# Gate and up products of a SwiGLU layer as Strassen block products, with the activations split later

## The chip, the cores and the metric

The kernel runs on one core of one Trainium2 chip. The metric is the time of one execution on the device, in microseconds (us). TensorE (PE in the rows) multiplies; VectorE (DVE), ScalarE (ACT) and GpSimd (POOL) work element by element; SyncE (SP) issues the loads of the weights.

## The reference, cut to what matters

One encoder layer over 512 tokens, model width 1024, inner width 2816, all in float32:

```python
h = h + 0.5 * swiglu(rms_norm(h, ffn1_norm), ffn1_w_gate, ffn1_w_up, ffn1_w_down)
u = rms_norm(h, mix_norm) @ w_in                  # 1024 -> 1280
...                                               # window attention and pooling on u
h = h + concat([a, p]) @ w_out
h = h + 0.5 * swiglu(rms_norm(h, ffn2_norm), ffn2_w_gate, ffn2_w_up, ffn2_w_down)
out = rms_norm(h, final_norm)

def swiglu(x, w_gate, w_up, w_down):
    return (silu(x @ w_gate) * (x @ w_up)) @ w_down
```

The change touches the two products `x @ w_gate` and `x @ w_up` of both FFNs, and how their result is handed to `w_down`.

## The kernel before

Every product is made from three matmuls in a 32-bit format of TensorE's that keeps fewer bits than float32 (fp32r in the rows). Each operand is split into a high part (a cast to that format, on ScalarE) and a low part (the rest, a subtraction on VectorE), and `mm3` (line 113) adds high times high, high times low and low times high into the same PSUM bank. Activations lie transposed, features on the 128 partitions and the 512 tokens along the free axis, so one matmul is 128x128 weights against 128x512 activations.

The weights come as a stream of *units* of 1 MB (a list `units`, line 56). `load` brings a unit into one of two `raw` buffers; `split_next` makes of each half of it, a *piece* of 1024 columns, the pair `wh`, `wl` (lines 97 and 98), in four buffers each; `weights()` hands out the next piece and keeps two more asked for. The code is run once to write the program down; each engine then takes its instructions strictly in its own order and waits by semaphores, and that order comes from the order of the code and a scheduler that may move an instruction ahead.

An FFN has two stages. In `gate_up` (line 202) the first three of the 22 column tiles (`F0 = 3`, each 128 inner columns of gate and of up) are done side by side over the eight blocks of the input as these become ready; this is the *head*, eight steps of 18 matmuls. At its end `norm_sums` (line 183) and `norm_spread` (line 197) make `rstd`, the factor of the RMS norm per token. Then follow 19 tiles of 2 x 8 x 3 = 48 matmuls each. The norm's factor is put in after the product: `glu` (line 203) multiplies the gate's bank by `rstd` on VectorE (line 206), takes the sigmoid on ScalarE (207), multiplies on GpSimd (208), multiplies the up bank in on VectorE (209) and `rstd` on GpSimd (210); then it splits the activation into high (ScalarE, 212) and low (GpSimd, 213), and both parts of all 22 tiles are kept. In `down` (line 250) each of the 22 blocks of `w_down` meets the kept parts in eight banks, 24 matmuls per block.

Between the two FFNs lies the mixing stage (projections, attention, pooling), which the change does not touch. Attention's scores are the only matmuls before that are 256 columns wide (lines 518 and 519).

Of the kernel before, what the change touches and what calls it, by code (L numbers as in the profile page):

```python
# [8 lines left out]
F32 = mybir.dt.float32  # L9
# [27 lines left out]
def encoder_layer(ctx: ExitStack, tc: tile.TileContext, xT, w1h, w1gu, w1d, win, wout, w2h, w2gu, w2d,  # L37
# [20 lines left out]
    units += [(w2gu, i) for i in range(NF - F0)] + [(w2d, i) for i in range(NF // 2)]  # L58
    stream = {"asked": 0, "raw": None, "ready": []}

    early = {}

    def load(i, between=None):
        src, j = units[i]
        n = src.shape[-1] // 2
        if i in early:
            return early.pop(i)
        raw = wts.tile([P, 2048], F32, name="raw", tag="raw", bufs=2)
        if i == 0:
# [6 lines left out]
        return raw, n  # L76

    def split_next():

        i, half = stream["asked"] // 2, stream["asked"] % 2  # L80
        if i == len(units):
            return
        if half == 0 and i:
            stream["raw"] = load(i)
        raw, n = stream["raw"]
        src = raw[:, half * n:(half + 1) * n]
        spare = stream.get("spare")
        if spare:
            wh, wl = spare.pop(0)
# [3 lines left out]
        m = n // 2 if stream["asked"] == 0 else n  # L93
        on_pool = WIN_POOL if units[i][0] is win else WOUT_POOL if units[i][0] is wout else ()
        sub = nc.gpsimd if 2 * units[i][1] + half in on_pool else nc.vector
        for c in range(0, n, m):
            nc.scalar.copy(wh[:, c:c + m], src[:, c:c + m])  # L97
            sub.tensor_tensor(wl[:, c:c + m], src[:, c:c + m], wh[:, c:c + m].bitcast(F32),  # L98
                              op=ALU.subtract)
        stream["asked"] += 1  # L100
        stream["ready"].append((wh, wl))

    def weights(ahead=2):
        while len(stream["ready"]) <= ahead and stream["asked"] < 2 * len(units):
            split_next()
        return stream["ready"].pop(0)
# [24 lines left out]

    stream["raw"] = load(0, start)
    nc.vector.memset(ones, 1.0)
# [3 lines left out]
    keep_awake(ps, WARM)  # L137
    early[1] = load(1)
    xload(4, 5, 6, 7)
# [60 lines left out]


    def gate_up(xh, xl, act, tmp, after_first, before=None, each=None):
        def glu(f, pg, pu):
            t1 = tmp.tile([P, S], F32, name="t1", tag="t1", bufs=2)
            t2 = tmp.tile([P, S], F32, name="t2", tag="t2", bufs=2)
            nc.vector.tensor_tensor(t1, pg, rstd, op=ALU.mult)  # L206
            nc.scalar.activation(t2, t1, AF.Sigmoid)  # L207
            nc.gpsimd.tensor_tensor(t2, t2, t1, op=ALU.mult)  # L208
            nc.vector.tensor_tensor(t1, pu, t2, op=ALU.mult)  # L209
            nc.gpsimd.tensor_tensor(t1, t1, rstd, op=ALU.mult)  # L210
            ah, al = act(f)
# [20 lines left out]
        after = after_first()  # L232
        for f in range(F0, NF):
            pb = []
            for u in range(2):
                wh, wl = weights()
                ps = bank()
                for k in range(KD):
                    c = slice(k * P, (k + 1) * P)
                    mm3(ps, wh[:, c], wl[:, c], xh[:, k, :], xl[:, k, :], k == 0, k == KD - 1)  # L240
                    if f == F0 and u == 0 and k == 4:
                        norm_spread(after)
                        for j in range(F0):
                            glu(j, banks[j], banks[F0 + j])
                pb.append(ps)
            glu(f, pb[0], pb[1])
            if each is not None:
                each(f)

    def down(act, tokens_first, finish):  # L250

        banks = [bank() for _ in range(8)]

        def one(i, k, wh, wl, last):
            ah, al = act(k)
            if tokens_first:
# [5 lines left out]

        kept, hold = [], 4 if tokens_first else 2
        for k in range(NF):
            if tokens_first and stream["asked"] == 2 * len(units) - 2:
                w2 = base.tile([P, 4, 1024], F32R, name="w2", tag="xl")
                stream["spare"] = [(w2[:, 0, :], w2[:, 1, :]), (w2[:, 2, :], w2[:, 3, :])]
            wh, wl = weights()
            if k < NF - hold:
                for i in range(8):  # L270
                    one(i, k, wh, wl, False)
            else:
                kept.append((k, wh, wl))
        for i in range(8):
            for k, wh, wl in kept:
                one(i, k, wh, wl, k == NF - 1)
            finish(i, banks[i])


    with tc.tile_pool(name="ffn1", bufs=1) as fp:  # L280
        a1h = fp.tile([P, NF, S], F32R, name="a1h")
        a1l = fp.tile([P, NF, S], F32R, name="a1l")

        def first_norm(k):

            norm_in(0, k, xh, xl)
            if k >= LAG:
                squares(k - LAG)

        def first_sums():  # L290
            for k in range(KD - LAG, KD):
                squares(k)
            return norm_sums()

        gate_up(xh, xl, lambda f: (a1h[:, f, :], a1l[:, f, :]), fp, first_sums,
                before=first_norm)
        yh = base.tile([P, KD, S], F32R, name="yh", tag="xh")
        yl = base.tile([P, KD, S], F32R, name="yl", tag="xl")

        def finish1(i, ps):  # L300
            nc.vector.scalar_tensor_tensor(h[:, i, :], ps, 0.5, h[:, i, :], op0=ALU.mult, op1=ALU.add)
            norm_in(1, i, yh, yl)

        down(lambda f: (a1h[:, f, :], a1l[:, f, :]), False, finish1)

# [330 lines left out]

    with tc.tile_pool(name="ffn2", bufs=1) as fp:
        FB = NF - 4
        a2h = fp.tile([P, FB, S], F32R, name="a2h")
        a2l = fp.tile([P, FB, S], F32R, name="a2l")  # L640
        hT = fp.tile([P, NT, D], F32, name="hT")
        late = []

        def after_first():
            spread = norm_sums()
            return spread

        def turn_h(f):
            if f <= F0:
                return  # L650
            if f - F0 - 1 < 2 * NT:
# [141 lines left out]
```

## Time and profile before

| | |
|---|---|
| time, median of 3 runs (lowest to highest) | 891.41 us (889.97 to 891.98) |
| the profiled execution's own time | 891.37 us |
| its span in the trace | 889.6 us |
| TensorE busy | 98% of the span, 3918 matmuls |
| VectorE, ScalarE, GpSimd busy | 46%, 35%, 35% |
| weights read | 82 MB, 95 GB/s over the span |

The span runs from the first to the last instruction that the profiler saw; the time of the execution is 1.8 us longer. "Busy" for TensorE counts matmuls in flight, which overlap. In the rows an instruction stands as start, duration, engine, line, operation and tiles (output <- inputs), and in brackets the idle time ahead of it and what ended that.

### The profile page before, as it was taken

How to read it: one execution, taken by the hardware profiler on the slowest of the kernel's cores; microseconds unless marked ns; L12 is line 12 of the kernel's file. 1: busy time of each engine (PE TensorE's matmuls, PEld its weight loads, DVE VectorE, ACT ScalarE, POOL GpSimd, SP SyncE). 2: the span in 40 equal slices, each digit the busy share in tenths (PEclk: the TensorE clock that was granted, in tenths of full speed). 3: DMA queues.
4: the chain of work that ended last, by engine and by line, in shares of the span. 5: the costliest groups of instructions: out<-in, count | busy, mean ns of one | idle time of the engine just before them, and what ended most of it. 6: DMA issues, size and time to landing. Idle time of an engine off the chain costs nothing.

```text
span 889.6 us, 9675 instructions
## 1 busy us (share of the span) xinstructions
PE 872.2 (98%) x3918; PEld 719.3 (81%) x3918; DVE 408.4 (46%) x516; ACT 309.9 (35%) x454; POOL 311.8 (35%) x255
## 2 busy tenths in 40 slices
PE   8999999999999999999789999999999999999996
PEld 7888888888888888887668888888888888888885
DVE  6444444444432221669887643444444444322225
ACT  7353222333321111543666532533323322211223
POOL 5186444444420001855542220763444444200004
PEclk9999999999999999999999999999999999999998
DMA  6422222222222222221211123122222222332202
GB/s 237 156 81 95 95 97 98 102 106 101 104 102 95 95 95 95 84 95 50 97 44 36 61 93 125 66 95 95 94 95 95 95 94 95 127 104 104 105 11 94
DMA packets 14683, 84.79 MB, mean 95 GB/s; under 512 B 1824, under 2 KB 2352, under 8 KB 5808
## 3 DMA queue, kind: packets, MB, share of 16 engines
q1 hardware_dynamic: 13104, 81.60, 25.8%
q10 hardware_dynamic: 1440, 2.57, 0.9%
q8 instruction: 30, 0.49, 0.2%
q14 instruction: 13, 0.11, 0.0%
q0 software_dynamic: 96, 0.02, 0.0%
HBM read 82.08 MB, written 2.10 MB: 95 GB/s over the span
## 4 chain that ended last, share of the span: by engine, by line
PE 92%; DVE 4%; ACT 1%; POOL 1%; issue 1%; DMA 0%; DVEq 0%; POOLq 0%; ACTq 0%
PE ps L114 29%; PE ps L115 29%; PE ps L116 29%; DVE qq L391 1%; PE ps L547 1%; DVE wl L98 1%; PE ps L563 1%; PE ps L562 1%; DVE rtmp L359 1%; DMA small<-in_gains 0%; PE ps L655 0%; DVE u L360 0%; PE ps L226 0%; PE ps L228 0%; PE ps L198 0%
## 5 line engine op out<-in xcount | busy, mean ns | idle before, releaser
L98 DVE TENSOR_TENSOR wl<-raw,wh 128x1024 fp32r<-128x1024 f32 (+2 forms) x146 | 215.6, 1478 | 206.2 <-ACT wh L97 197.7
L97 ACT CAST wh<-raw 128x1024 fp32r<-128x1024 f32 (+2 forms) x153 | 156.3, 1024 | 415.1 <-PE ps L115 339.3
L114 PE MATMUL ps<-zh,wh 128*128 128x512 f32 x346 | 135.5, 392 | 0.0
L115 PE MATMUL ps<-zl,wh 128*128 128x512 f32 x346 | 135.1, 390 | 0.0
L116 PE MATMUL ps<-xh,wl 128*128 128x512 f32 x346 | 135.0, 391 | 0.0
L114 PE MATMUL ps<-xh,wh 128*128 128x512 f32 x346 | 134.8, 390 | 0.0
L116 PE MATMUL ps<-zh,wl 128*128 128x512 f32 x346 | 134.8, 390 | 0.0
L115 PE MATMUL ps<-xl,wh 128*128 128x512 f32 x346 | 134.6, 389 | 0.0
L208 POOL TENSOR_TENSOR t<-t,t 128x512 f32<-128x512 f32 x44 | 77.7, 1769 | 146.0 <-ACT t L207 146.0
L210 POOL TENSOR_TENSOR t<-t,rstd 128x512 f32<-128x512 f32 x44 | 61.2, 1394 | 99.3 <-DVE t L209 99.3
L209 DVE TENSOR_TENSOR t<-ps,t 128x512 f32<-128x512 f32 x44 | 30.4, 691 | 120.2 <-PE ps L116 108.2
L114 PEld LDWEIGHTS ps<-xh,wh 128*128 128x128 f32 x346 | 64.9, 188 | 13.9 <-ACT wh L97 0.2
L116 PEld LDWEIGHTS ps<-zh,wl 128*128 128x128 f32 x346 | 64.9, 188 | 13.9 <-issue 0.2
L116 PEld LDWEIGHTS ps<-xh,wl 128*128 128x128 f32 x346 | 64.9, 188 | 14.0 <-issue 0.2
L115 PEld LDWEIGHTS ps<-zl,wh 128*128 128x128 f32 x346 | 65.0, 188 | 13.4 <-issue 0.2
L115 PEld LDWEIGHTS ps<-xl,wh 128*128 128x128 f32 x346 | 65.0, 188 | 13.4
L114 PEld LDWEIGHTS ps<-zh,wh 128*128 128x128 f32 x346 | 65.0, 188 | 13.2
L206 DVE TENSOR_TENSOR t<-ps,rstd 128x512 f32<-128x512 f32 x44 | 30.2, 691 | 92.3 <-PE ps L116 75.9
L114 PE MATMUL ps<-a1h,wh 128*128 128x512 f32 x176 | 68.5, 389 | 0.0
L115 PE MATMUL ps<-a1l,wh 128*128 128x512 f32 x176 | 68.5, 389 | 0.0
L116 PE MATMUL ps<-a1h,wl 128*128 128x512 f32 x176 | 68.5, 389 | 0.0
L98 POOL TENSOR_TENSOR wl<-raw,wh 128x1024 fp32r<-128x1024 f32 x7 | 16.8, 2396 | 117.3 <-ACT wh L97 114.3
(189 smaller groups left out, 1270.2 us busy)
## 6 DMA issues: line engine op xcount, KB each, us to landing
raw<-in_w1gu SPq DMA_DIRECT2D x19, 1024.0 KB, 4.7
raw<-in_w2gu SPq DMA_DIRECT2D x19, 1024.0 KB, 4.7
raw<-in_w1d SPq DMA_DIRECT2D x11, 1024.0 KB, 4.7
raw<-in_w2d SPq DMA_DIRECT2D x11, 1024.0 KB, 4.8
raw<-in_win SPq DMA_DIRECT2D x5, 1024.0 KB, 4.7
raw<-in_wout SPq DMA_DIRECT2D x4, 1024.0 KB, 4.8
raw<-in_w2h SPq DMA_DIRECT2D x4, 768.0 KB, 4.2
raw<-in_w1h SPq DMA_DIRECT2D x3, 768.0 KB, 4.3
```

The source lines that it names most:

```text
L97: nc.scalar.copy(wh[:, c:c + m], src[:, c:c + m])
L98: sub.tensor_tensor(wl[:, c:c + m], src[:, c:c + m], wh[:, c:c + m].bitcast(F32), op=ALU.subtract)
L114: nc.tensor.matmul(ps, lhsT=ah, rhs=bh, start=start, stop=False)
L115: nc.tensor.matmul(ps, lhsT=ah, rhs=bl, start=False, stop=False)
L116: nc.tensor.matmul(ps, lhsT=al, rhs=bh, start=False, stop=stop)
L206: nc.vector.tensor_tensor(t1, pg, rstd, op=ALU.mult)
L208: nc.gpsimd.tensor_tensor(t2, t2, t1, op=ALU.mult)
L209: nc.vector.tensor_tensor(t1, pu, t2, op=ALU.mult)
L210: nc.gpsimd.tensor_tensor(t1, t1, rstd, op=ALU.mult)
L359: nc.vector.tensor_tensor(rot, rot, sr, op=ALU.mult)
L391: nc.vector.scalar_tensor_tensor(t[o, :], u[r, :], -HD ** -0.5, t[r, :].bitcast(F32), op0=ALU.mult, op1=ALU.subtract)
L547: nc.tensor.transpose(ps[:, i * P:(i + 1) * P], sc[g][0][:, i, (b - lo) * P:(b - lo + 1) * P], ident)
```

## The change

For 37 of the 38 later tiles (18 in FFN1, where one tile stays as it was, and 19 in FFN2; the constant `PLAIN`) the gate and up columns of one tile are taken as a 2x2 block product: the weights in four blocks of 512 rows by 128 columns (a11 and a12 are gate's two halves of the input rows, a21 and a22 up's), the activations in four blocks of 512 rows by 256 tokens. Strassen's scheme in Winograd's form needs seven block products where the plain way needs eight. A block product is 4 x 3 matmuls of 128x128 weights against 128x256 activations, so a tile has 84 matmuls of 256 columns in place of 48 of 512.

- The four sums of the weights are made per tile in a buffer `sums`, of which there is one: three on GpSimd (lines 106, 107 and 111), one on VectorE (114). A unit now gives four pieces (three of 1024 columns, one of 512) to cast and subtract.
- The four sums of the input are made once per FFN, in `combine`, four rounds of two products with gain and `rstd` on VectorE (line 248), four subtractions on GpSimd (251), one cast of 1792 columns on ScalarE (252) and one subtraction of the same width on VectorE (253). Its buffer has the tag of `sums`. So that `rstd` is there in time, `norm_sums` and `norm_spread` move into the head (`norm_steps`).
- The seven products are added up by four instructions on VectorE that read PSUM (lines 320, 323, 326 and 330) and a copy on ScalarE (316). The activation is one SiLU on ScalarE and one product on GpSimd (333).
- The activations are kept whole, and `down` splits each block two ahead of its use, on ScalarE and VectorE (lines 391 and 392).

```diff
+            a11, a12, a21, a22 = (raw[:, c * 512:(c + 1) * 512] for c in range(4))
+            if part == 0:
+                stream["sums"] = stream["pool"].tile([P, 2048], F32, name="sums", tag="sums")
+            s2, s1, s3, s4 = (stream["sums"][:, c * 512:(c + 1) * 512] for c in range(4))
+            n = 512 if part == 3 else 1024
+            if part == 0:
+                nc.gpsimd.tensor_tensor(s1, a21, a22, op=ALU.add)
+                nc.gpsimd.tensor_tensor(s3, a11, a21, op=ALU.subtract)
+                src = raw[:, 0:1024]
+            elif part == 1:
+                load(i + 1)
+                nc.gpsimd.tensor_tensor(s2, s1, a11, op=ALU.subtract)
+                src = stream["sums"][:, 0:1024]
+            elif part == 2:
+                nc.vector.tensor_tensor(s4, a12, s2, op=ALU.subtract)
+                src = stream["sums"][:, 1024:2048]
+            else:
+                src = a22
...
+        def combine(j):
+
+            b = gp.tile([P, 2048], F32, name="tt", tag="sums").rearrange("p (b c) -> p b c", b=8)
+            for k, o in ((j, b[:, 0:8:7, :]), (j + KD // 2, b[:, 1:3, :])):
+                nc.vector.scalar_tensor_tensor(o, halves(h[:, k, :]), gain[:, n, k:k + 1], halves(rstd),
+                                               op0=ALU.mult, op1=ALU.mult)
+            for o, x, y in ((3, 7, 0), (5, 2, 7), (4, 2, 3), (6, 1, 4)):
+                nc.gpsimd.tensor_tensor(b[:, o, :], b[:, x, :], b[:, y, :], op=ALU.subtract)
+            nc.scalar.copy(th[:, j, :, :], b[:, 0:7, :])
+            nc.vector.tensor_tensor(tl[:, j, :, :], b[:, 0:7, :], th[:, j, :, :].bitcast(F32),
+                                    op=ALU.subtract)
...
+        def product(w, side, t, ps):
+            for j in range(KD // 2):
+                c = slice(side * 512 + j * P, side * 512 + (j + 1) * P)
+                mm3(ps, w[0][:, c], w[1][:, c], th[:, j, t, :], tl[:, j, t, :], j == 0, j == KD // 2 - 1)
+
+        for f in range(F0 + PLAIN[0 if n == 0 else 1], NF):
+
+            c = parts()
+            b0, b1 = halves(bank()), halves(bank())
+            w = weights()
+            product(w, 0, 0, b0[:, 0, :])
+            p1 = gp.tile([P, 1, HF], F32, name="p1", tag="p1")
+            nc.scalar.copy(p1[:, 0, :], b0[:, 0, :])
+            product(w, 1, 1, b1[:, 0, :])
+            w = weights()
+            product(w, 0, 4, b1[:, 1, :])
+            nc.vector.tensor_tensor(c[:, 0:6:5, :], b1, p1.to_broadcast([P, 2, HF]), op=ALU.add)
+            v = weights()
+            product(v, 0, 5, b0[:, 1, :])
+            nc.vector.tensor_tensor(c[:, 4, :], b0[:, 1, :], c[:, 5, :], op=ALU.add)
+            b2, b3 = halves(bank()), halves(bank())
+            product(w, 1, 3, b2[:, 0:1, :])
+            nc.vector.tensor_tensor(c[:, 3:7:3, :], c[:, 4:6, :], b2[:, 0:1, :].to_broadcast([P, 2, HF]),
+                                    op=ALU.add)
+            product(v, 1, 2, b3[:, 1, :])
+            product(weights(), 0, 6, b3[:, 0, :])
+            nc.vector.tensor_tensor(c[:, 1:3, :], b3, c[:, 4:7:2, :], op=ALU.add)
+            t2 = pair("t2")
+            nc.scalar.activation(halves(t2), c[:, 0:4:2, :], AF.Silu)
+            nc.gpsimd.tensor_tensor(halves(act(f)), c[:, 1:4:2, :], halves(t2), op=ALU.mult)
+            each(f)
...
+        ab[0], ab[1] = split(0), split(1)
         for k in range(NF):
             wh, wl = weights()
+            if 0 < k < NF - 1:
+                ab[k + 1] = split(k + 1)
...
+            nc.scalar.copy(ah, act(k))
+            nc.vector.tensor_tensor(al, act(k), ah.bitcast(F32), op=ALU.subtract)
```

Below, the four pieces of a tile are called 0 to 3 in the order of the code, the sums s1 to s4 as in the code, the VectorE instructions that add up the products c1 to c4 in the order of the code (lines 320, 323, 326, 330). The products run in the order t = 0, 1, 4, 5, 3, 2, 6; piece 0 serves the first two, piece 1 the third and fifth, piece 2 the fourth and sixth, piece 3 the last.

VectorE's order, before, over two tiles in the middle of FFN1 (names with a number are `glu`'s buffers):

```order
L206 TENSOR_TENSOR t_1076<-ps,rstd 128x512
L98 TENSOR_TENSOR wl<-raw,wh 128x1024
L209 TENSOR_TENSOR t_1076<-ps,t_1077 128x512
L98 TENSOR_TENSOR wl<-raw,wh 128x1024
L206 TENSOR_TENSOR t_1145<-ps,rstd 128x512
L98 TENSOR_TENSOR wl<-raw,wh 128x1024
L209 TENSOR_TENSOR t_1145<-ps,t_1146 128x512
L98 TENSOR_TENSOR wl<-raw,wh 128x1024
```

The same engine now, from one tile's c1 to the next one's (`parts` holds the tile's partial sums, `p` with a number is the copy p1):

```order
L320 TENSOR_TENSOR parts<-ps,p_1245 128x2x256
L323 TENSOR_TENSOR parts<-ps,parts 128x256
L326 TENSOR_TENSOR parts<-parts,ps 128x2x256
L126 TENSOR_TENSOR wl<-sums,wh 128x1024 x2
L330 TENSOR_TENSOR parts<-ps,parts 128x512
L126 TENSOR_TENSOR wl<-raw,wh 128x512
L114 TENSOR_TENSOR sums<-raw,sums 128x512
L126 TENSOR_TENSOR wl<-raw,wh 128x1024
L320 TENSOR_TENSOR parts<-ps,p_1366 128x2x256
```

Four instructions per tile became nine: c1 to c3 of a tile, then pieces 1 and 2 of the next tile, c4, piece 3 of the next tile, then s4 and piece 0 of the tile after that.

GpSimd's order, before, over two tiles of FFN1:

```order
L208 TENSOR_TENSOR t_870<-t_870,t_869 128x512
L210 TENSOR_TENSOR t_869<-t_869,rstd 128x512
L213 TENSOR_TENSOR a1l<-t_869,a1h 128x512
L208 TENSOR_TENSOR t_939<-t_939,t_938 128x512
L210 TENSOR_TENSOR t_938<-t_938,rstd 128x512
L213 TENSOR_TENSOR a1l<-t_938,a1h 128x512
```

And now (`late_xh` holds the kept activations):

```order
L106 TENSOR_TENSOR sums<-raw 128x512
L107 TENSOR_TENSOR sums<-raw 128x512
L111 TENSOR_TENSOR sums<-sums,raw 128x512
L333 TENSOR_TENSOR late_xh<-parts,t_1343 128x512
L106 TENSOR_TENSOR sums<-raw 128x512
L107 TENSOR_TENSOR sums<-raw 128x512
L111 TENSOR_TENSOR sums<-sums,raw 128x512
```

Three instructions per tile became four, and the product of the activation stands behind the three sums of a later tile.

VectorE's order now where FFN1's input is summed, after the head (L248 and L253 are `combine`; L258, L263 and L392 belong to the head's activations):

```order
L248 SCALAR_TENSOR_TENSOR tt<-h,small,rstd 128x2x256
L248 SCALAR_TENSOR_TENSOR tt<-h,small,rstd 128x512
L263 TENSOR_TENSOR parts<-ps,t_399 128x512
L258 TENSOR_TENSOR parts<-ps,rstd 128x512
L392 TENSOR_TENSOR as_2557<-some,as_2557 128x512 x2
L253 TENSOR_TENSOR tl<-tt,th 128x1792
L263 TENSOR_TENSOR parts<-ps,t_493 128x512
L114 TENSOR_TENSOR sums<-raw,sums 128x512
L126 TENSOR_TENSOR wl<-sums,wh 128x1024 x2
L126 TENSOR_TENSOR wl<-raw,wh 128x512
L248 SCALAR_TENSOR_TENSOR tt<-h,small,rstd 128x2x256
L248 SCALAR_TENSOR_TENSOR tt<-h,small,rstd 128x512
```

These are the second round and the start of the third; the first block tile's weight sums, which use the same buffer, stand between them.

## Rows read from the trace of the kernel before

**Rows 1.** The page's first part: busy time, share of span, instructions.
```profile
PE 872.2 (98%) x3918; PEld 719.3 (81%) x3918; DVE 408.4 (46%) x516; ACT 309.9 (35%) x454; POOL 311.8 (35%) x255
```

**Rows 2.** Timeline, one tile of FFN1: VectorE, then GpSimd (start us, duration us).
```profile
101.67 0.69 DVE L206 TENSOR_TENSOR t<-ps,rstd 128x512 f32<-128x512 f32 x1 [2.23 <-PE ps L116]
102.57 1.23 DVE L98 TENSOR_TENSOR wl<-raw,wh 128x1024 fp32r<-128x1024 f32 x1 [0.21 <-ACT wh L97]
107.18 0.69 DVE L209 TENSOR_TENSOR t<-ps,t 128x512 f32<-128x512 f32 x1 [3.38 <-PE ps L116]
108.02 2.30 DVE L98 TENSOR_TENSOR wl<-raw,wh 128x1024 fp32r<-128x1024 f32 x1
112.55 0.69 DVE L206 TENSOR_TENSOR t<-ps,rstd 128x512 f32<-128x512 f32 x1 [2.23 <-PE ps L116]
...
107.95 1.29 POOL L210 TENSOR_TENSOR t<-t,rstd 128x512 f32<-128x512 f32 x1 [3.00 <-DVE t L209]
109.97 1.49 POOL L213 TENSOR_TENSOR a1l<-t,a1h 128x512 fp32r<-128x512 f32 x1 [0.73 <-ACT a1h L212]
```

**Rows 3.** Timeline of TensorE in the mixing stage: matmuls of 256 columns.
```profile
467.95 0.28 PE L518 MATMUL ps<-kk,qq 128*128 128x256 f32 x1
...
468.43 0.39 PE L114 MATMUL ps<-pdh,wh 128*128 128x512 f32 x1
```

**Rows 4.** Timeline of FFN1's head: VectorE, then GpSimd.
```profile
19.30 1.09 DVE L98 TENSOR_TENSOR wl<-raw,wh 128x768 fp32r<-128x768 f32 x1 [0.87 <-ACT wh L97]
20.32 2.04 DVE L98 TENSOR_TENSOR wl<-raw,wh 128x768 fp32r<-128x768 f32 x1
...
19.66 1.88 POOL L171 TENSOR_TENSOR acc<-acc,sq 128x512 f32<-128x512 f32 x1
```

**Rows 5.** Timeline after FFN1's head: VectorE with a PSUM operand, then GpSimd.
```profile
59.30 0.68 DVE L209 TENSOR_TENSOR t<-ps,t 128x512 f32<-128x512 f32 x1
...
56.99 3.53 POOL L208 TENSOR_TENSOR t<-t,t 128x512 f32<-128x512 f32 x2 [0.20 <-ACT t L207]
```

**Rows 6.** Groups by line and shape: count, busy us, mean ns, idle before.
```profile
L98 POOL TENSOR_TENSOR wl<-raw,wh 128x1024 fp32r<-128x1024 f32 x7 | 16.8, 2396 | 117.3 <-ACT wh L97 114.3 <-PE ps L114 3.0
L403 DVE TENSOR_TENSOR vv<-ps,vv 128x256 fp32r<-128x256 f32 x2 | 0.8, 410 | 0.0
L97 ACT CAST wh<-raw 128x1024 fp32r<-128x1024 f32 x136 | 143.0, 1052 | 398.3 <-PE ps L115 325.9 <-PE ps L116 65.8 <-POOL acc L171 3.5
L97 ACT CAST wh<-raw 128x768 fp32r<-128x768 f32 x15 | 12.3, 835 | 14.7 <-PE ps L115 13.4 <-PE ps L226 0.7 <-DMA raw<-in_w1h 0.5
```

**Rows 7.** Timeline of VectorE: 512 columns, both operands in SBUF.
```profile
419.32 0.68 DVE L359 TENSOR_TENSOR rtmp<-rtmp,sr 128x512 f32<-128x512 f32 x1
```

**Rows 8.** Timeline, marks of both FFNs: two head steps (VectorE), then TensorE.
```profile
28.58 1.23 DVE L98 TENSOR_TENSOR wl<-raw,wh 128x1024 fp32r<-128x1024 f32 x1 [2.29 <-ACT wh L97]
32.66 1.23 DVE L98 TENSOR_TENSOR wl<-raw,wh 128x1024 fp32r<-128x1024 f32 x1 [2.85 <-ACT wh L97]
...
39.77 0.95 PE L187 MATMUL ps<-ones,acc 128*128 128x1 f32 x8
248.35 0.39 PE L114 MATMUL ps<-a1h,wh 128*128 128x512 f32 x1
517.82 0.39 PE L224 MATMUL ps<-zh,wh 128*128 128x512 f32 x1
551.27 0.49 PE L114 MATMUL ps<-zh,wh 128*128 128x512 f32 x1
762.91 0.39 PE L114 MATMUL ps<-wh,a2h 128*128 128x512 f32 x1
```

**Rows 9.** Timeline of TensorE at the start of attention's scores, after a wait.
```profile
430.32 0.39 PE L518 MATMUL ps<-kk,qq 128*128 128x256 f32 x1 [2.49 <-DVE qq L391]
...
431.31 0.63 PE L115 MATMUL ps<-yl,wh 128*128 128x512 f32 x1
431.74 0.63 PE L116 MATMUL ps<-yh,wl 128*128 128x512 f32 x1
```

More of the change, by code (lines that the diff above doesn't have):

```diff
@@ L58, in encoder_layer @@
     units += [(w2gu, i) for i in range(NF - F0)] + [(w2d, i) for i in range(NF // 2)]
-    stream = {"asked": 0, "raw": None, "ready": []}
-    early = {}
+    pieces = []
+    for i, (src, j) in enumerate(units):
+        if (src is w1gu and j >= PLAIN[0]) or (src is w2gu and j >= PLAIN[1]):
+            pieces += [("block", i, part) for part in range(4)]
+        else:
+            pieces += [("half", i, 0), ("half", i, 1)]
+    stream = {"asked": 0, "ready": []}
+    raws = {}
     def load(i, between=None):
+        if i in raws or i == len(units):
+            return
         src, j = units[i]
         n = src.shape[-1] // 2
-        if i in early:
-            return early.pop(i)
         raw = wts.tile([P, 2048], F32, name="raw", tag="raw", bufs=2)
-        if i == 0:
+        raws[i] = raw
+        if between is not None:
             for q in range(4):
@@ L103, in weights @@
     def weights(ahead=2):
-        while len(stream["ready"]) <= ahead and stream["asked"] < 2 * len(units):
+        while len(stream["ready"]) <= ahead and stream["asked"] < len(pieces):
             split_next()
@@ L130, in start @@
         xload(*((0,), (1,), (2,), (3,))[q])
-    stream["raw"] = load(0, start)
+    load(0, start)
     nc.vector.memset(ones, 1.0)
@@ L240, in gate_up, with down @@
                     mm3(ps, wh[:, c], wl[:, c], xh[:, k, :], xl[:, k, :], k == 0, k == KD - 1)
[L241 to L244, printed above, removed]
                 pb.append(ps)
[L246 to L250, printed above, removed]
+                after(KD + u, combine)
+            glu_up(f, pb[1], *glu_gate(pb[0]))
+        def product(w, side, t, ps):
[27 more added lines that the diff above has]
+            each(f)
+    def down(split, tokens_first, finish, ready=None):
         banks = [bank() for _ in range(8)]
+        ab = {}
         def one(i, k, wh, wl, last):
-            ah, al = act(k)
+            ah, al = ab[k]
             if tokens_first:
@@ L273, in down @@
                 kept.append((k, wh, wl))
+        if ready is not None:
+            ready()
         for i in range(8):
@@ L277, in down, with inner, act, split @@
             finish(i, banks[i])
+    def inner(first, pool, place):
+        some = pool.tile([P, 6, S], F32, name="some")
+        late, done = {}, {}
+        def act(f):
+            if f < 6:
+                return some[:, f, :]
+            t = ("xh", "xl")[(f - 6) // 8]
+            if t not in late:
+                late[t] = base.tile([P, 8, S], F32, name="late_" + t, tag=t)
+            return late[t][:, (f - 6) % 8, :]
+        def split(k, where=None):
+            if k in done:
+                return done[k]
+            if k < 2:
+                if "place" not in done:
+                    done["place"] = place()
+                ah, al = (done["place"][:, 2 * k + c, :] for c in range(2))
+            else:
+                t = where.tile([P, 2, S], F32R, name="as", tag="as", bufs=6)
+                ah, al = t[:, 0, :], t[:, 1, :]
+            nc.scalar.copy(ah, act(k))
+            nc.vector.tensor_tensor(al, act(k), ah.bitcast(F32), op=ALU.subtract)
+            done[k] = ah, al
+            return done[k]
+        return act, split
@@ L280, in encoder_layer @@
     with tc.tile_pool(name="ffn1", bufs=1) as fp:
-        a1h = fp.tile([P, NF, S], F32R, name="a1h")
-        a1l = fp.tile([P, NF, S], F32R, name="a1l")
+        act1, split1 = inner(True, fp, lambda: fp.tile([P, 4, S], F32R, name="as0"))
         def first_norm(k):
[L286 to L296, printed above, removed]
@@ L634, in encoder_layer @@
             weave(project_out(d, ath, atl, finish_attn), [])
[L637 to L640, printed above, removed]
+    with ExitStack() as two:
+        fp = two.enter_context(tc.tile_pool(name="ffn2", bufs=1))
         hT = fp.tile([P, NT, D], F32, name="hT")
[L642 to L646, printed above, removed]
+        act2, split2 = inner(False, fp, lambda: base.tile([P, 4, S], F32R, name="as0", tag="h"))
         def turn_h(f):
```

139 lines of the change are left out of this document (87 added, 52 removed).

## The prediction

> **What bounds the kernel now.** I read the busy shares first: TensorE 98%, the three element-wise engines 35 to 46% [rows 1]. Then one tile: the same VectorE line comes at 101.67 and 112.55 [rows 2], so a tile takes 10.88 us, and 48 matmuls in 10.88 us are 0.227 us each. TensorE sets the pace, and the others wait for it (the brackets name PE). Then I read how VectorE and GpSimd stand to each other, since the change puts its additions there. At 108.02 a 1024-column subtraction with both operands in SBUF takes 2.30 us in place of the 1.23 us of 102.57: GpSimd had begun 0.07 us before it and held until 109.24, and 1.08 us later VectorE was done. The other way round, GpSimd's line 213 begins at 109.97 and ends at 111.46, 1.14 us after VectorE's end at 110.32, where line 210 alone takes 1.29 [rows 2]. So two such instructions do not overlap at all; one waits until the other has ended. Back to back they take turns: VectorE's two of 19.30 and 20.32 let GpSimd's in between, which ends 21.54 (1.15 after 20.39), and the second ends 0.82 after that [rows 4]. An instruction of VectorE with a PSUM operand is free of this: 0.68 us at 59.30 inside a pair of GpSimd's [rows 5].
>
> **TensorE's part.** Per block tile 48 matmuls of 512 go and 84 of 256 come. Four of 256 columns, each with its own weights, start within 467.95 to 468.43 [rows 3], 0.120 each; half of 0.227 would be 0.113. I take 0.118, so 84 x 0.118 = 9.9 us (bounds 9.5 and 10.1): 1.0 us less per tile, 37 us over 37 tiles, if nothing else sets the pace. The Trainium skill (TensorE: Matmul & The Clock Gate, Back-to-back issue gap) gives 262 cycles at full clock for 256 columns, 0.109 us, which would make the tile 9.2 us; its 518 cycles for 512 are 0.216, where this trace has 0.227, so the rows are taken; by the page's figure rival (a) below would be 25 us shorter and the forecast the same.
>
> **The tile on VectorE and GpSimd.** There is one buffer `sums`. s1 of the next tile but one can start only when the subtraction of piece 2 has read it, and VectorE's order ties the rest: s4 needs s2, piece 0 stands behind s4, c1 to c3 behind piece 0, pieces 1 and 2 behind c3. That is a ring, and it turns once per tile. Its prices: GpSimd, 512 columns, 1.29, or 1.14 after a wait for VectorE [rows 2]; VectorE, 1024 columns, 1.23 with a pitch of 1.14 (estimate: 0.08 of the next overlaps, as 20.32 begins 0.07 before 20.39 [rows 4]), 512 columns in SBUF 0.68 [rows 7], 0.54 after a wait (half of 1.08), c1 and c3 like the 0.69 of line 209 [rows 2], c2 the 0.41 of 256 columns [rows 6]. From the end of piece 2:
> s1 0.08 + 1.29; piece 3, which waited for s1, 0.54; s3, which waited for piece 3, 1.14; s2 1.29; then the product of the activation, next on GpSimd and long ready, 1.29; s4, which waited for that, 0.54; piece 0 1.14; c1, c2, c3 0.69 + 0.41 + 0.69; pieces 1 and 2 1.14 + 1.23. Sum **11.47**; some steps overlap by hundredths and I take **11.4 us** per tile. c4 runs beside s1 and costs nothing. TensorE's products for c1 to c3 are long done by then: the third begins when piece 1 is ready, a whole turn ahead. So the ring is 1.5 us longer than TensorE's 9.9, and longer than the old 10.88. Lower bound 10.9, with every GpSimd step at 1.14; upper 11.7, with 0.08 more at each handoff.
>
> **The start of each FFN.** A round of `combine`: two products with two SBUF operands, 2 x 0.68; four GpSimd subtractions of 256 columns, not in the trace: from 1.29 at 512 and 2.40 at 1024 [rows 2, 6] the line gives 0.74, half of 1.29 gives 0.65, I take 0.74 and 2.96; a cast of 1792, by the line through 0.84 and 1.05 at 768 and 1024 [rows 6], 1.70; a subtraction of 1792, by the line through 0.68 and 1.23 [rows 2, 7], 2.05. With handoffs 8.2 us, and since the rounds share the one buffer they follow each other: 33 us (bounds 28 and 38).
> FFN1: a head step is 4.08 us [rows 8], two before the head's end at 39.77 are left after the sums, so the spread is done at 37.4 and `rstd` at 38.4. Rounds from 39, 33 us, and between the second and third the first block tile's sums and pieces (3 x 1.29, 0.68, 2.3 and a cast ahead, 8 us), and 1 us of the head's own work: the last round ends at 81. By the order 44 of the tile's 84 matmuls need it: 5.2 us, the first block tile ends at **86**. Before, 17 tiles of 10.88 end at 248.35 [rows 8], so that one ended at 63.4: 23 us lost. Tile two's sums begin at 81 (same buffer); its piece 2 is ready 10.3 us later (3 x 1.29, s4, three pieces, c1 to c4), four products follow, 5.7 us: **97**. Sixteen more tiles: 97 + 16 x 11.4 = 279.4 against 248.35, **+31**.
> FFN2: there is no plain tile as cover. Sums after two head steps, spread after three, `rstd` at 517.82 + 14.8 = 532.6. Rounds to 567; s1, s3, a product of the head's, s2, s4, piece 1: 574; five products, 7.1: the first block tile ends at **581** where the old one ended about 562.5 (551.27 [rows 8] + 10.88 and 0.4 of the norm's spread). The second, whose sums follow at once, at 588; 17 more: 588 + 17 x 11.4 = 781.8 against 762.91 [rows 8], **+19**.
>
> **What hides.** The split in `down`: 0.62 (the casts' line at 512) and 0.68 per block beside 5.44 us of TensorE, with 1.05 and 1.23 there already; GpSimd is idle there, so nothing is waited for. If that cover went it would be 44 x 0.7 us = 31 us. Loads: a raw buffer is free one turn ahead of its need. c4, SiLU, the copy p1: beside the ring. The moved sums of the norm: the same matmuls, elsewhere. I take 0 for these, with -2 to +4.
>
> **Sum.** 889.6 + 31 + 19 = 939.6 us of span, 941.4 with the 1.8 us around it; the profiled execution (891.37) is the median's (891.41) within 0.1 us. Forecast **941**, its own range 920 (ring 10.9, 33 turns, -16; starts -5) to 957 (ring 11.7, +10; starts +6).
>
> **Rivals.** (a) *The ring does not bind.* If VectorE and GpSimd overlap here as they do with PSUM [rows 5], the ring loses piece 3's 0.54 and the product's 1.29, comes to 9.8, and TensorE's 9.9 sets the tile; the starts stay. FFN1 86 + 17 x 9.9 = 254.3 (+6); FFN2 581 + 18 x 9.9 + 4 for the transposes of h that stand between the tiles (762.91 - 551.27 is 4.9 more than 19 x 10.88) = 763 (0): **897**. For it: only pairs of VectorE and GpSimd were seen, not the new shapes. Against: no two-SBUF pair in the rows overlaps.
> (b) *Faster.* The rounds hide too, because the first tile's products start on the rounds that are done. Then 37 x 1.0 us come off: **857**. It decides from the point at which the last round ends before TensorE has run out of plain work (52 us in FFN1, 552 in FFN2); by the sum it ends at 81 and 567, so both rounds' prices would have to halve.
> (c) *Slower still, by the clock.* After a wait of 2.49 us TensorE's matmuls of 512 stand 0.43 apart, which is 1.2 GHz, where they stood 0.23 apart before [rows 9]. In the ring TensorE waits 1.5 us a turn. If it fell to the lower level in each turn and stayed, 84 x 0.215 = 18 us per tile, 33 x 6.7 = 221 more: 1160; if for a short stretch only, hidden in the wait. It decides from waits as long as the row's 2.49.
> (d) *It does not do what it says*, the tiles as before: 891. The order shows the 84 products, so this is left at nothing.
>
> **How the numbers follow.** Forecast 0.70, (a) 0.13, (b) 0.11, (c) 0.06, of it most above 957. The range 895 to 957 takes in the forecast's and (a): about 0.8. A measurement of this kernel tells 0.2% (1.8 us) from no change. Faster: (b) and a little of (a), 0.14; the same: a part of (a), 0.04; slower: the rest, 0.82.
>
> **What the changed kernel's profile would show.** c1 of successive tiles 11.4 us apart on VectorE, GpSimd's four in a row with s4 starting only at the end of line 333; TensorE's idle time in front of the third product, ended by VectorE's `wl` of piece 1, about 1.5 us a tile, and TensorE near 85% in these stretches. In the ramps TensorE idle around 55 to 80 and 555 to 575, ended by line 253. Tiles 9.9 us apart would speak for (a); a first block tile that ends near 62 and 562 for (b); a granted clock at half for (c). The prediction is wrong if the two engines overlap, if GpSimd's 256-column prices are far off, or if TensorE's 256-column matmuls need more than 0.135 us, so that it bounds again.

## The result and the profile after

The changed kernel takes 954.33 us (median of four runs, 954.25 to 955.12) against 891.27 us for the kernel before (889.97 to 891.98): a ratio of 1.071, 95% interval 1.069 to 1.073. It is slower, by 63 us. The profiled execution has a span of 952.6 us, 13.0 us above the 939.6 of the prediction's sum.

The page's busy shares of the changed kernel, the lines that answer to [rows 1]:

```profile
PE 868.1 (91%) x5250; PEld 772.9 (81%) x5250; DVE 608.2 (64%) x769; ACT 390.4 (41%) x573; POOL 350.8 (37%) x310
```

TensorE is no longer busy throughout, and no other engine has come near 100%: no engine's work alone sets the pace, but an order of waits. Three groups of the page say which (after the bar: busy us, mean ns; then the idle time ahead and what ended it):

```profile
L141 PE MATMUL ps<-th,wh 128*128 128x256 f32 x1036 | 301.0, 292 | 61.7 <-ACT p L316 34.0
L106 POOL TENSOR_TENSOR sums<-raw 128x512 f32<-128x512 f32 x37 | 48.4, 1309 | 201.6 <-DVE wl L126 189.6
L114 DVE TENSOR_TENSOR sums<-raw,sums 128x512 f32<-128x512 f32 x37 | 61.1, 1653 | 92.3 <-POOL sums L111 92.3
```

GpSimd's s1 waits for VectorE's piece 2, VectorE's s4 waits for GpSimd's s2: each engine idles for the other. One turn in the middle of FFN1, VectorE and then GpSimd (start us, duration us), where [rows 2] showed one tile of before:

```profile
155.72 0.68 DVE L320 TENSOR_TENSOR parts<-ps,p 128x512 f32<-128x512 f32 x1
156.50 0.42 DVE L323 TENSOR_TENSOR parts<-ps,parts 128x256 f32<-128x256 f32 x1
157.03 0.69 DVE L326 TENSOR_TENSOR parts<-parts,ps 128x512 f32<-128x512 f32 x1
157.63 2.35 DVE L126 TENSOR_TENSOR wl<-sums,wh 128x1024 fp32r<-128x1024 f32 x2
159.90 0.68 DVE L330 TENSOR_TENSOR parts<-ps,parts 128x512 f32<-128x512 f32 x1
160.50 1.43 DVE L126 TENSOR_TENSOR wl<-raw,wh 128x512 fp32r<-128x512 f32 x1
164.38 1.76 DVE L114 TENSOR_TENSOR sums<-raw,sums 128x512 f32<-128x512 f32 x1 [2.44 <-POOL sums L111]
166.06 1.21 DVE L126 TENSOR_TENSOR wl<-raw,wh 128x1024 fp32r<-128x1024 f32 x1
167.20 0.68 DVE L320 TENSOR_TENSOR parts<-ps,p 128x512 f32<-128x512 f32 x1
...
160.12 1.27 POOL L106 TENSOR_TENSOR sums<-raw 128x512 f32<-128x512 f32 x1 [6.01 <-DVE wl L126]
161.34 1.75 POOL L107 TENSOR_TENSOR sums<-raw 128x512 f32<-128x512 f32 x1
163.05 1.29 POOL L111 TENSOR_TENSOR sums<-sums,raw 128x512 f32<-128x512 f32 x1
164.30 1.29 POOL L333 TENSOR_TENSOR late_xh<-parts,t 128x512 f32<-128x512 f32 x1
```

From c1 (line 320) at 155.72 to c1 at 167.20 are 11.48 us. The ends read as a chain: piece 2 at 159.98, s1 161.39, piece 3 161.93 (begun at 160.50, stretched to 1.43 because s1 was running), s3 163.09, s2 164.34, the product 165.59, s4 166.14 (begun at 164.38, stretched to 1.76 behind the product), piece 0 167.27. c4 at 159.90, which reads PSUM, runs beside s1 and stretches neither. TensorE's turn at the same place, and ScalarE's ahead of it:

```profile
161.56 0.38 PE L141 MATMUL ps<-th,wh 128*128 128x256 f32 x1 [1.15 <-ACT p L316]
161.78 0.28 PE L142 MATMUL ps<-tl,wh 128*128 128x256 f32 x1
161.90 0.28 PE L143 MATMUL ps<-th,wl 128*128 128x256 f32 x1
...
160.62 0.63 ACT L332 ACTIVATE t<-parts 128x512 f32<-128x512 f32 x1 [3.93 <-DVE parts L330]
161.16 0.35 ACT L316 COPY p<-ps 128x256 f32<-128x256 f32 x1
```

Matmuls of 256 columns start 0.120 us apart, 84 x 0.120 = 10.08 us; the rest of the 11.48 is one pause of 1.4 us per tile (1.15 of them waiting for the copy p1).

The marks of the stages, TensorE's first matmul of FFN1's down stage, of FFN2's head, of FFN2's down stage:

```profile
282.29 0.40 PE L141 MATMUL ps<-as,wh 128*128 128x512 f32 x1
551.78 0.39 PE L274 MATMUL ps<-zh,wh 128*128 128x512 f32 x1
823.26 0.40 PE L141 MATMUL ps<-wh,as 128*128 128x512 f32 x1
```

Against [rows 8]: gate and up of FFN1 end 33.9 us later (282.29 - 248.35); FFN1's down stage and the mixing take 269.49 where they took 269.47; FFN2's head and tiles take 271.48 where they took 245.09, 26.4 more; from there to the span's end 129.3 where it was 126.7, 2.7 more. 33.9 + 26.4 + 2.7 = 63.0 us, the whole loss.

### The profile page after: what moved, and what is told of

Same layout as the page of the kernel before. It is cut to its first block, busy times and chain, and to the rows that moved or that the text cites. A ratio compares the mean times of both kernels' runs of the same rounds, so it can differ in the third digit from the quotient of the medians.

```text
span 952.6 us, 13092 instructions
## 1 busy us (share of the span) xinstructions
PE 868.1 (91%) x5250; PEld 772.9 (81%) x5250; DVE 608.2 (64%) x769; ACT 390.4 (41%) x573; POOL 350.8 (37%) x310
## 5 line engine op out<-in xcount | busy, mean ns | idle before, releaser
L141 PE MATMUL ps<-th,wh 128*128 128x256 f32 x1036 | 301.0, 292 | 61.7 <-ACT p L316 34.0
L142 PE MATMUL ps<-tl,wh 128*128 128x256 f32 x1036 | 297.9, 288 | 6.4 <-DVE tl L253 6.4
L143 PE MATMUL ps<-th,wl 128*128 128x256 f32 x1036 | 296.5, 287 | 0.6 <-DVE wl L126 0.6
L126 DVE TENSOR_TENSOR wl<-raw,wh 128x1024 fp32r<-128x1024 f32 (+3 forms) x146 | 184.1, 1263 | 147.5 <-ACT wh L125 141.0
L141 PEld LDWEIGHTS ps<-th,wh 128*128 128x128 f32 x1036 | 201.8, 196 | 70.4 <-ACT p L316 40.4
L125 ACT CAST wh<-raw 128x1024 fp32r<-128x1024 f32 (+3 forms) x153 | 140.2, 919 | 184.8 <-PE ps L142 112.6
L142 PEld LDWEIGHTS ps<-tl,wh 128*128 128x128 f32 x1036 | 202.9, 196 | 7.7 <-DVE tl L253 7.7
L143 PEld LDWEIGHTS ps<-th,wl 128*128 128x128 f32 x1036 | 202.5, 196 | 0.9 <-DVE wl L126 0.8
L141 PE MATMUL ps<-as,wh 128*128 128x512 f32 x176 | 68.5, 389 | 0.0
L142 PE MATMUL ps<-as,wh 128*128 128x512 f32 x176 | 68.5, 389 | 0.0
L143 PE MATMUL ps<-wh,as 128*128 128x512 f32 x160 | 63.0, 394 | 0.0
L141 PE MATMUL ps<-wh,as 128*128 128x512 f32 x160 | 63.0, 394 | 0.0
```

The source lines that it names most:

```text
L125: nc.scalar.copy(wh[:, c:e], src[:, c:e])
L126: sub.tensor_tensor(wl[:, c:e], src[:, c:e], wh[:, c:e].bitcast(F32), op=ALU.subtract)
L141: nc.tensor.matmul(ps, lhsT=ah, rhs=bh, start=start, stop=False)
L142: nc.tensor.matmul(ps, lhsT=ah, rhs=bl, start=False, stop=False)
L143: nc.tensor.matmul(ps, lhsT=al, rhs=bh, start=False, stop=stop)
```

## Experiments

**Does TensorE or the ring set the tile? The sums left out.**

```diff
-                nc.gpsimd.tensor_tensor(s1, a21, a22, op=ALU.add)
-                nc.gpsimd.tensor_tensor(s3, a11, a21, op=ALU.subtract)
...
-                nc.gpsimd.tensor_tensor(s2, s1, a11, op=ALU.subtract)
-                src = stream["sums"][:, 0:1024]
+                src = raw[:, 512:1536]
...
-                nc.vector.tensor_tensor(s4, a12, s2, op=ALU.subtract)
-                src = stream["sums"][:, 1024:2048]
+                src = raw[:, 1024:2048]
```

> Leaves out the four sums of the weights (s1 to s4); pieces 1 and 2 are cut from the raw buffer instead. All 84 matmuls, casts, subtractions and the rounds of the input's sums stay. Theory (the ring over the one buffer sets the tile): s1, s3, s2, s4 fall away, so TensorE sets the tile at 84 x 0.120 = 10.1 us; 33 tiles x 1.4 us less, 954 - 46 = 908 us, a little less still because the second tile of each FFN need not wait for the rounds' buffer. Rival (TensorE's 256-column products set the tile): c1 stays 11.5 us apart, about 950. Rival (all of VectorE's and GpSimd's work, whatever its order, sets the tile): four sums of 512 less, about 4.4 us, so TensorE's 10.1 as well; this run does not tell that one apart.

This kernel leaves the sums out, so its products are not the layer's; it is a measure of time alone. Measured: 898.54 us (one run), beside 891.12 for the kernel before in the same session. c1 of two successive tiles (line 313 there):

```profile
159.83 0.68 DVE L313 TENSOR_TENSOR parts<-ps,p 128x512 f32<-128x512 f32 x1
169.91 0.68 DVE L313 TENSOR_TENSOR parts<-ps,p 128x512 f32<-128x512 f32 x1
```

10.08 us: TensorE can do it, and does not set the 11.48. The total fell by 56 us, 10 more than the 46 expected: 26.9 us in FFN1's gate and up and 27.4 in FFN2's, where 16 and 17 turns of 1.41 are 22.6 and 24.0; the rest lies at the starts, in FFN2's one longer tile (below) and 1.6 us between FFN1's down stage and FFN2's head, which this edit did not touch and which took 267.9 to 270.9 us over all runs. It is not the prediction's rival (a), where the sums stay and the engines overlap, but it answers the same question: even with a ring that doesn't bind, the starts eat the gain. That it comes near (a)'s 897 is in part chance, since (a) keeps the starts as they are.

**The length of the ring, step by step: the product moved.**

```diff
-            nc.gpsimd.tensor_tensor(halves(act(f)), c[:, 1:4:2, :], halves(t2), op=ALU.mult)
+            nc.vector.tensor_tensor(halves(act(f)), c[:, 1:4:2, :], halves(t2), op=ALU.mult)
```

> Only the product of the activation goes from GpSimd to VectorE; the sums stay where they are. Theory (the ring holds that product as a step of 1.29 us between s2 and s4): s4 follows s2 at once, 1.29 go, and the product comes back as 0.68 on VectorE beside s1: 10.7 to 10.9 us from c1 to c1, 33 x 0.7 = 23 less, about 931. Rival (TensorE's wait for the copy p1 on ScalarE sets the tile): 11.5 as before, 954. Rival (VectorE's added work is in the ring in full and more, because it waits for s1 or s3): 11.5 to 12.2, 954 to 980.

Measured: 933.50 us (one run). GpSimd's s3 and s2, then VectorE's c1, the product, s4 and the next c1:

```profile
157.57 1.74 POOL L107 TENSOR_TENSOR sums<-raw 128x512 f32<-128x512 f32 x1
159.27 1.74 POOL L111 TENSOR_TENSOR sums<-sums,raw 128x512 f32<-128x512 f32 x1
...
151.91 0.69 DVE L320 TENSOR_TENSOR parts<-ps,p 128x512 f32<-128x512 f32 x1
...
158.08 1.78 DVE L333 TENSOR_TENSOR late_xh<-parts,t 128x512 f32<-128x512 f32 x1
161.05 0.69 DVE L114 TENSOR_TENSOR sums<-raw,sums 128x512 f32<-128x512 f32 x1 [1.19 <-POOL sums L111]
...
162.79 0.69 DVE L320 TENSOR_TENSOR parts<-ps,p 128x512 f32<-128x512 f32 x1
```

10.88 us from c1 to c1. The product's turn has moved between s3 and s2 (it waits for s3, s2 waits for it) and costs half as much there; s4 now lasts 0.69, not 1.76. The 0.6 us that a step of 1.25 loses when it becomes one of 0.6 came off the tile in full, so the product was in the ring. The edit touched neither the copy p1 nor the SiLU ahead of it; TensorE's wait behind p1 fell from 1.15 to 0.54 us, by as much as the tile: that wait takes up what the ring leaves, it does not set the pace.

**The same for the three sums, all on VectorE.**

```diff
-                nc.gpsimd.tensor_tensor(s1, a21, a22, op=ALU.add)
-                nc.gpsimd.tensor_tensor(s3, a11, a21, op=ALU.subtract)
+                nc.vector.tensor_tensor(s1, a21, a22, op=ALU.add)
+                nc.vector.tensor_tensor(s3, a11, a21, op=ALU.subtract)
...
-                nc.gpsimd.tensor_tensor(s2, s1, a11, op=ALU.subtract)
+                nc.vector.tensor_tensor(s2, s1, a11, op=ALU.subtract)
```

> s1, s3 and s2 go from GpSimd to VectorE; one buffer, all else the same. Theory (the ring's length is the sum of its steps, GpSimd's 1.29 and the handoffs among them): three GpSimd steps of 1.14 to 1.29 become VectorE steps of about 0.6, the ring comes to 11.5 - 3 x 0.6 = 9.7, so TensorE sets the tile at 10.1 to 10.4 us; 33 x 1.2 = 40 less, about 914. Rival (TensorE): 11.5, 954. Rival (VectorE, now the engine with most work, 9.3 us of its own and up to 1.2 of waiting for GpSimd's product): 10.5, so 33 x 1.0 less, about 921.

Measured: 907.19 us (one run), 7 less than the 914 expected, mainly because each turn lost 1.4 us and not 1.2. From s1 to c1, then the one instruction that GpSimd keeps:

```profile
160.36 0.69 DVE L106 TENSOR_TENSOR sums<-raw 128x512 f32<-128x512 f32 x1
160.97 1.78 DVE L107 TENSOR_TENSOR sums<-raw 128x512 f32<-128x512 f32 x1
162.67 0.68 DVE L111 TENSOR_TENSOR sums<-sums,raw 128x512 f32<-128x512 f32 x1
163.39 0.69 DVE L114 TENSOR_TENSOR sums<-raw,sums 128x512 f32<-128x512 f32 x1
164.00 0.68 DVE L320 TENSOR_TENSOR parts<-ps,p 128x512 f32<-128x512 f32 x1
174.09 0.68 DVE L320 TENSOR_TENSOR parts<-ps,p 128x512 f32<-128x512 f32 x1
...
160.65 1.55 POOL L333 TENSOR_TENSOR late_xh<-parts,t 128x512 f32<-128x512 f32 x1 [8.51 <-ACT t L332]
```

The four sums take 3.7 us (160.36 to 164.08) where the ring took 6.2 for them, piece 3 and the product (159.98 to 166.14), and the tile is 10.09: TensorE sets it again, with one buffer for the sums as before. VectorE does more work in this kernel than in the changed one (650.0 us busy against 608.2), and the kernel is 47 us faster. The edit does two things at once, it halves three steps and takes the handoffs between them out; this run does not tell them apart. The Trainium skill (GPSIMD Engine Reference, Engine selection) gives additions on a tile to VectorE, about twice as fast for two inputs; the rows agree, 0.69 against 1.27.

**Is it the one buffer? Two buffers for the sums, in FFN1 alone.**

```diff
-                stream["sums"] = stream["pool"].tile([P, 2048], F32, name="sums", tag="sums")
+                stream["sums"] = stream["pool"].tile([P, 2048], F32, name="sums", tag="sums",
+                                                     bufs=stream["bufs"])
```

> Two buffers for the weights' sums (and the rounds) in FFN1 alone; FFN2 keeps one and is the control in the same execution. Theory (the one buffer closes the ring): FFN1's tiles fall from 11.49 to TensorE's 10.1 us or up to 10.4, FFN2's stay 11.49; 16 x 1.2 = 19 us less, and the rounds of FFN1 may overlap by some us: about 930. Rival (the sum of VectorE's and GpSimd's work sets the tile, taking turns, the instructions that read PSUM included): 4 x 1.2 of GpSimd, 0.54 + 0.54 + 3 x 1.14 of VectorE, 2.5 for c1 to c4 give 11.8, so FFN1's tiles stay at 11.5 and the time at 950 or more.

Measured: 956.86 us (one run); FFN2's tiles 11.49, FFN1's 12.3, which neither had said. VectorE and GpSimd in FFN1 (its lines are one higher), in a turn that took 13.2 us because its load was late:

```profile
169.80 0.69 DVE L115 TENSOR_TENSOR sums<-raw,sums 128x512 f32<-128x512 f32 x1 [4.63 <-POOL sums L112]
170.41 1.22 DVE L127 TENSOR_TENSOR wl<-sums,wh 128x1024 fp32r<-128x1024 f32 x1
...
166.01 1.29 POOL L107 TENSOR_TENSOR sums<-raw 128x512 f32<-128x512 f32 x1 [4.98 <-DMA raw<-in_w1gu]
```

With a buffer free, the scheduler put the next tile's s4 ahead of this tile's piece 2 on VectorE. s4 now waits 4.63 us (3.69 in the turn ahead) for sums whose weights have just landed, and SyncE issues that load only when VectorE's subtraction of piece 3 has read its raw buffer. So the second buffer made a ring through the raw buffers in place of the one through `sums`. Whether two buffers in the old order would have helped, this run does not tell; it stays open. That the one buffer alone does not bind, the run before shows.

**The starts: four plain tiles as cover.**

```diff
-PLAIN = (1, 0)
+PLAIN = (4, 4)
...
-                after(KD + u, combine)
+                after(KD + 2 * (f - F0) + u, combine)
             glu_up(f, pb[1], *glu_gate(pb[0]))
+            each(f)
```

> Four plain tiles in each FFN instead of one and none, so that the rounds of the input's sums run beside 43.5 us of plain products; 15 block tiles remain in each. Theory (the starts are lost because TensorE runs out of plain work at 52 and 552 us while the rounds go on to 81 and 601): with plain work to 83 in FFN1 and 76 us after FFN2's start the idle stretches and the half clock go; FFN1's gate and up end at 39.8 + 43.5 + 15 x 11.49 = 256 instead of 282, FFN2's take 33 + 43.5 + 172 = 249 to 253 instead of 271.5; about 907 us. Rival (the plain tiles' own pieces and norms on VectorE push the rounds back by as much as they cover): the first block tile still waits 5 us or more in each FFN, 917 or more.

Measured: 907.81 us (one run); FFN1's gate and up end at 258.5, FFN2's take 248.5. The stretches of the starts, of the changed kernel, then of this one (length, busy us of PE, PEld, DVE, ACT, POOL, granted clock, DMA share, GB/s):

```profile
56.00:82.00 26.00, 9.60 (x34) 7.83 (x35) 13.12 (x12) 5.98 (x5) 11.81 (x13) 0.50 0.11 41
82.00:86.50 4.50, 4.50 (x23) 4.50 (x22) 1.23 (x2) 1.32 (x2) 3.23 (x3) 0.50 0.00 0
86.50:90.00 3.50, 3.50 (x30) 3.50 (x29) 3.29 (x5) 2.35 (x3) 0.00 (x0) 0.95 0.00 0
```

```profile
56.00:84.00 28.00, 28.00 (x125) 23.20 (x124) 18.73 (x17) 9.50 (x11) 16.09 (x13) 1.00 0.20 76
576.00:597.00 21.00, 21.00 (x98) 17.40 (x97) 12.48 (x12) 8.80 (x10) 11.50 (x9) 1.00 0.28 101
```

TensorE was idle for 16 of 26 us and is busy throughout; the half clock is gone with the waits. 46.5 us came back, about 4 of them because seven more tiles are plain, and the cover cost nothing, since a plain tile (10.88) is shorter than a block tile of this kernel (11.49).

**The last 2.7 us: whole activations, and where their split lies.** One kernel has plain tiles only and keeps the activations whole (`PLAIN = (19, 19)`, `some` for all 22, no sums); the other changes only the place of the split in FFN2's down stage:

```diff
-            if k < 2:
+            if k < 2 or not first:
                 if "place" not in done:
                     done["place"] = place()
-                ah, al = (done["place"][:, 2 * k + c, :] for c in range(2))
+                q = k % 4
+                ah, al = (done["place"][:, 2 * q + c, :] for c in range(2))
```

> All 38 tiles plain (48 matmuls of 512 columns), no sums of weights or input; but the activations are kept whole and split in the down stage, as in the changed kernel. Theory (the split in the down stage is hidden): 891 us as before, FFN1's down stage and the mixing unchanged. Rival (the 2.7 us by which FFN2's down stage grew belong to the split): 893 to 894, with the matmuls of FFN2's down stage 0.231 apart instead of 0.227.

> In FFN2's down stage the split activations of all 22 blocks go to four slots where h was, instead of six slots in that stage's own pool (where h was they lie only for the first two blocks); the same splits at the same places, all else as in the changed kernel. Theory (where the 128x128 operand lies in SBUF sets the 0.232 us between matmuls from the third block on): all blocks at 0.227 as the first two, the down stage 126.7 us instead of 129.3, 951.7 in all. Rival (the splits on ScalarE and VectorE beside the matmuls slow them): 0.232 stays, 954.3.

Measured, one run each: 893.54 us for plain tiles (before: 891.12), with gate and up of FFN1 ending at 249.5 and 129.3 us from FFN2's down stage to the end; 952.96 us for the other place, its down stage 127.1, 2.2 less than in the changed kernel, of which 1.4 show in the total (FFN2's tiles took 1.0 longer, which was not followed up). The totals alone are too close to tell; the stage and its spacing do. Sixty microseconds of that stage: before, the changed kernel, plain tiles, other place (PE's count first in the brackets):

```profile
783.00:843.00 60.00, 60.00 (x267) 49.67 (x266) 13.47 (x11) 11.61 (x11) 0.00 (x0) 1.00 0.27 89
```

```profile
844.00:904.00 60.00, 60.00 (x260) 48.66 (x259) 19.88 (x22) 17.27 (x22) 0.00 (x0) 1.00 0.25 88
```

```profile
782.50:842.50 60.00, 60.00 (x260) 48.66 (x259) 19.21 (x21) 17.27 (x22) 0.00 (x0) 1.00 0.24 88
```

```profile
844.20:904.20 60.00, 60.00 (x267) 49.72 (x266) 21.10 (x22) 17.31 (x22) 0.00 (x0) 1.00 0.26 89
```

260 matmuls in 60 us are 0.231 each, 267 are 0.225 (the count takes in those in flight at the ends; from start to start the rows have 0.232 and 0.227), at the same clock and with the same splits beside them in the last three. So the splits cost nothing in that stage; the place of the 128x128 operand did (with it the number of slots changed, from six to four). The last four blocks still stood 0.230 apart in the other place, 0.4 us that were not followed up.

**Together.** Sums on VectorE, four plain tiles, the other place (the three diffs above).

> s1 to s3 on VectorE, four plain tiles in each FFN, and the split activations of FFN2 where h was, together. If the three causes are apart: FFN1's gate and up end at 39.8 + 43.5 + 15 x 10.08 = 234.5 us (248.35 in the kernel before), FFN2's take 33 + 43.5 + 151 + up to 4 = 228 to 232 (245.1 before), the last down stage 126.7: 861 to 868 us, 3% faster than the kernel before. If VectorE's longer list takes the place of the ring once tiles follow without a pause (10.5 a tile): 874 to 880.

Measured: 868.15 us (866.85 to 870.74, four runs) against 892.02 (889.65 to 893.60, seven runs): a ratio of 0.9735, interval 0.9705 to 0.9765. It beats both kernels. It lies at the upper edge of the 861 to 868 expected: FFN1's gate and up end at 236.9 (234.5 expected), FFN2's take 232.8, the last down stage 127.0. The busy shares, c1 of two tiles on VectorE, and TensorE's first matmul of two tiles:

```profile
PE 850.0 (98%) x4998; PEld 753.7 (87%) x4998; DVE 610.1 (70%) x824; ACT 377.8 (44%) x552; POOL 215.6 (25%) x199
```

```profile
153.04 0.69 DVE L321 TENSOR_TENSOR parts<-ps,p 128x512 f32<-128x512 f32 x1
163.01 0.68 DVE L321 TENSOR_TENSOR parts<-ps,p 128x512 f32<-128x512 f32 x1
...
146.21 0.28 PE L141 MATMUL ps<-th,wh 128*128 128x256 f32 x1
156.29 0.28 PE L141 MATMUL ps<-th,wh 128*128 128x256 f32 x1
```

TensorE sets the pace again, at 10.08 us a tile, its matmuls 0.120 apart without a pause. VectorE's c1 come 9.97 apart because VectorE, which never waits in this stretch, is still catching up; read from c1 alone, the tile would seem 0.11 us too short. 0.80 us per tile less than the 10.88 of before, on 30 tiles, are the 24 us that came. VectorE's list of 9.97 is so close behind that little more could be given to it.

## Why the prediction was right, step by step

The measured time lies 13 us above the forecast of 941, inside its own range of 920 to 957, but not by the terms that set the upper end: there 10 us were allowed for the ring, which gave 3, and 6 for the starts, which gave about 8; 2.7 came from the last down stage. That the ring binds, and its length, were right by their steps; that the total stayed inside the range is in part luck.

- **TensorE, 9.9 us a tile (bounds 9.5 and 10.1).** 10.08 where nothing else binds (the sums left out, the sums on VectorE, and the combined kernel); a spacing of 0.120, not 0.118. The Trainium skill's 262 cycles (TensorE: Matmul & The Clock Gate, Back-to-back issue gap), 0.109 us, was not seen over a tile in any run; the rows of attention's scores [rows 3] were the right source.
- **The ring, 11.47, taken as 11.4.** 11.48 to 11.49. By ends in the turn shown: s1 1.41 (1.37 forecast), piece 3 0.54 (0.54), s3 1.16 (1.14), s2 1.25 (1.29), product 1.25 (1.29), s4 0.55 (0.54), piece 0 1.13 (1.14), c1 to c3 1.93 (1.79), pieces 1 and 2 2.27 (2.37). That the two engines exclude each other, read from [rows 2, 4], holds for the pairs in that turn (s1 with piece 3, the product with s4), and that PSUM operands are free, from [rows 5], for c4. Most of the 33 x 0.09 = 3 us that the tiles are longer than forecast is the needless rounding from 11.47 to 11.4, 33 x 0.07.
- **What closes the ring.** The turn shows the sum term by term, and two runs that shortened steps shortened the tile as the sum says; the statement that the one buffer closes it is only half shown, since the second buffer changed the order.
- **The place of TensorE's wait.** Forecast ahead of the third product, ended by piece 1, 1.5 us. It lies ahead of the fourth, ended by the copy p1 behind the SiLU, 1.4 us with the pause around it. The size followed from the ring, the place did not; TensorE was busy 90% of the turn, where 85% was forecast. In the starts its waits were ended by the casts of line 252 (18 us in all) more than by line 253 (6 us), which was forecast alone.
- **FFN1's start, +31 with its ring.** +33.9. `rstd` and the rounds came as worked out: the last ends at 81.40 (81 forecast). But the first block tile's products end at 89.3, not 86: of the 44 matmuls left, 25 started 0.214 apart. At the granted 0.50 that is 1.2 GHz. What the term lacked is that TensorE, idle between the rounds, would begin its 44 at the lower level, 25 x 0.094 = 2.3 us. The second tile follows without a pause and ends at 99.3, not 97; the 16 turns behind it give the rest. Rival (c) had the mechanism, though for the wrong place: in the ring, with waits of 1.15 us, the clock stayed at 1.00.
- **FFN2's start and tiles, +19.** +26.4, the largest miss. The rounds end at 567.5 on the clock of before (567 forecast) and the five products begin at 573.6 (574); they end 2.1 us late, again at 1.2 GHz. The second tile ends at 593.6, not 588: the sum let it end 7 us after the first, though by the prediction's own price its 84 matmuls need 9.9; this step of the sum was wrong, and it makes 3.4 us. The 17 tiles behind add 2.0. Among them is one of 12.89 us (c1 at 706.77 and 719.66), in which the splits of the down stage's first two blocks stand on VectorE between GpSimd's sums:

```profile
713.27 1.78 DVE L392 TENSOR_TENSOR as<-some,as 128x512 fp32r<-128x512 f32 x1
```

- **What hides, 0 with -2 to +4.** The splits inside the down stage are hidden, as said; the two of FFN2 that come ahead of it are not, they cost that tile 1.4 us. FFN1's down stage and the mixing are unchanged (269.49 and 269.47; so near is chance, as the stage varies by 3 us between runs). The 2.7 us in FFN2's down stage are inside the bound, by a cause that was not in the list.
- **The rivals.** (a), that the engines overlap, is refuted by the turn: s1 stretched piece 3 to 1.43, the product stretched s4 to 1.76. (b) did not occur; four plain tiles in each FFN are enough cover, fewer were not tried. Its price is also off: 891.4 less 37 is 854, not 857.

## What to carry to other kernels

Before work goes to the engines that seem idle, write down one turn of the new loop as a chain of ends, with each handoff and each pair that cannot overlap: VectorE at 64% and GpSimd at 37% set the pace here, because nearly all of their work in a tile was one chain, each step behind the other engine's. Put the steps of such a chain on one engine, even on the busier one, if its list still fits into the pace (9.97 of 10.08 us here), and give a stage that must prepare something as much old work for cover as the preparation lasts. A second buffer is no cure by itself, since it can also change the order. And read the pace from the engine that sets it: another one may be catching up.

## What the runs showed of the hardware that had not been expected

- Matmuls whose 128x128 operand lies in one place of SBUF start 0.232 us apart on average, in another 0.227, at the granted 1.00, with no wait and the same work beside them. No run here tells which property of the address decides. The Trainium skill (SBUF — State Buffer, Who interferes with whom) has contention on the engines' side only between VectorE and GpSimd; this case's rows show TensorE's own pace changing with an operand's place.
- TensorE stayed at the granted 1.00 through a wait of 1.15 us in every tile. In FFN1's start it fell to 0.50 in the second of two waits, 2.24 us before 55.02 and 1.21 us before 57.08, and was back at 1.00 at 87, when it had run without a wait since 81.45:

```profile
55.00:56.00 1.00, 0.85 (x5) 0.65 (x5) 1.00 (x1) 0.50 (x1) 0.00 (x0) 1.00 0.00 0
57.00:58.00 1.00, 0.92 (x4) 0.93 (x4) 0.62 (x2) 0.00 (x0) 0.90 (x1) 0.50 0.00 0
```

The rows are windows of the changed kernel, the granted clock third from the end. So a wait of the same length let the clock fall in one place and not in another; what tells them apart, no run here was made to find.
